# RWKV-7 pairs: the second head's products of three steps on the other column half of TensorE, put back in place by the copies

## The chip, the cores and the metric

One core of one Trainium2 chip runs the whole program as one launch. The metric is the device time of one execution in microseconds (us). Five engines are named as the profile names them: PE (TensorE, matrix products; PEld are its weight loads), DVE (VectorE), ACT (ScalarE), POOL (GpSimd) and SP (which issues the DMAs). A matmul reads a stationary operand and a moving operand from SBUF and writes into one of eight PSUM banks; ACT or DVE then copies the result out.

## The reference

A decoder trunk of two layers over 512 tokens of width 1024. Each layer has a token mixer with three branches (sparse attention NSA, latent attention MLA, RWKV-7 time mixing), merged by gates, and a gated MLP behind it. The change touches the RWKV-7 branch alone: eight heads of width 64 with a state that is carried from token to token:

```python
def step(state, inp):
    r_t, d_t, k_t, v_t, kk_t, a_t = inp
    sa = jnp.einsum('bhij,bhj->bhi', state, -kk_t)
    state = (state * d_t[:, :, None, :] + sa[..., None] * (kk_t * a_t)[:, :, None, :]
             + v_t[..., None] * k_t[:, :, None, :])
    return state, jnp.einsum('bhij,bhj->bhi', state, r_t)
...
_, y = lax.scan(step, state0, xs)
```

The kernel computes the scan in chunks of 64 tokens. Within a chunk the token-by-token recurrence becomes a triangular system, so that nearly everything is a product of 64x64 matrices in f32.

## The kernel before

All instructions of the program come from generator functions ("tasks") that a list scheduler written in the kernel interleaves: at each step it gives the next place to the request that could start first by its own cost table, then by priority (a smaller number goes first). The scheduler fixes the order of each engine's instructions when the program is built. The large matrix products of the projections and the MLP are one task, `master` (priority 9), which walks a list of units in a fixed order (`ORDER`): it fills PE's time wherever the other tasks have nothing ready. Its weights come by DMA, are rounded to a high part by ACT (the CASTs of line 507 into `hlt`) and get a low part by DVE (line 476, `hlt<-rawt,hlt`).

Eight heads make four **pairs** per layer (`rwkv_pair`, spawned by `rwkv_setup`, priority 1, at most three alive at once), so eight pairs in all. A pair holds four blocks `t` of 128 tokens, each two chunks `c` of 64 tokens; chunk `c` lies on partitions 64c to 64c+63 (`cs(c)`). Head `h` of the pair lies along the free axis. The steps of a pair in their order:

- `chunk_mats(2, ..)` and, in the task `left`, `chunk_mats(3, ..)`: products within each chunk, `Ab` and `Ak`, 16 matmuls of 64x64 with 128 columns each. Then in `left`: **X1**, 16 matmuls `Ak` by `v4` with 64 columns, into one bank, copied out by ACT in one instruction.
- `rw_inverse`, beside `left`: inverts the triangular systems.
- **solve**, behind both: 2 tasks, one a head, 8 matmuls each with 128 columns into a bank of their own, copied to `G` with factor -0.5 by ACT or DVE, whichever the scheduler finds free first.
- `mat_rm` and `mat_k`: 32 matmuls each, written through `quad`; beside them **local** (priority 1.5): 32 matmuls (16 pairs that accumulate) into one bank, copied to `Yp` by ACT.
- a scan of six short steps over the chunks, the readout (16 matmuls through `quad`), normalisation, output.

`pe` hands matmuls to PE in pieces of 8, between which other tasks may come. `quad(a, b, 2)` takes two matmuls of list `a`, two of `b`, and so on. PE's array is used as four quadrants here: the partitions of the operands choose the row half, the partitions of the output the column half. In `chunk_mats`, `mat_rm`, `mat_k` and the readout four consecutive matmuls lie in four different quadrants. In X1, solve and local both operands lie on `cs(c)` and the output on `cs(c)` too, so that only the two quadrants on the diagonal are used, whatever the head.

Each f32 matmul stands in the trace as two MATMUL records: the 16 matmuls of X1 are x32, the 32 of local x64.

Of the kernel before, what the change touches and what calls it, by code (L numbers as in the profile page):

```python
# [429 lines left out]
class Kern:  # L430
# [1744 lines left out]
    def rwkv_pair(self, l, st, i):  # L2175
        nc, A = self.nc, self.A
        tts = range(4)
        idn = self.ident()
        name = self.sch.cur.name
# [10 lines left out]
        src = A["rwrow"][l, i]  # L2190
# [9 lines left out]
        cs = lambda c: slice(64 * c, 64 * c + 64)  # L2200
        AR = yield from self.pages(2, None, job)
        al, X1p = self.pg(AR), self.pg(AR + 1)
# [92 lines left out]
        pr = self.sch.cur.prio  # L2295
# [29 lines left out]
        v4 = vv.rearrange("p (t h c) -> p t h c", t=4, h=2)  # L2325
        ka4 = ka.rearrange("p (t h c) -> p t h c", t=4, h=2)
        bt4 = bt.rearrange("p (t h c) -> p t h c", t=4, h=2)
        alx = self.pg(AR, 2).rearrange("p (w t h c) -> p w t h c", w=2, t=4, h=2)
        hct = [(h, t, c) for t in tts for h in range(2) for c in range(2)]
# [3 lines left out]
        Ab = self.pg(AB, 2).rearrange("p (h t w c) -> p h t w c", h=2, t=4, w=2)  # L2333
        Ak = self.pg(AK, 2).rearrange("p (h t w c) -> p h t w c", h=2, t=4, w=2)

        def chunk_mats(q, M, mo):
            T = self.pg(CTs[q])
            bs, os, mm = [], [], [[], []]
            for h in range(2):
                bs.append((yield from self.bank()))  # L2340
                os.append(self.ps[bs[h]].rearrange("p (t w c) -> p t w c", t=4, w=2))
                for t in tts:
                    for c in range(2):
                        tk = slice(t * 128 + 64 * c, t * 128 + 64 * c + 64)
                        mm[h].append((os[h][64 * c:64 * c + 64, t], T[cs(h), tk], arT[cs(h), :, tk], True, True))
            yield from self.quad(*mm, 2)
            for h in range(2):
                self.fork()
                yield from self.tt(M[:, h], os[h], self.kc(mo, 128).rearrange("p (w c) -> p w c", w=2)[:, None]
                                   .to_broadcast([128, 4, 2, 64]), OP.mult)  # L2350
                self.bfree(bs[h])
            self.join()

        yield dn[0]
        yield dn[1]
        self.pfree(P["rho"])

        def left():
            yield dn[3]
            yield from chunk_mats(3, Ak, KP_MK)  # L2360
            self.pfree(CT3)

            b = yield from self.bank()
            o = self.ps[b].rearrange("p (t h c) -> p t h c", t=4, h=2)
            mm = [(o[cs(c), t, h], Ak[cs(c), h, t, 0], v4[cs(c), t, h], True, True) for h, t, c in hct]
            yield from self.pe(mm[:8])
            yield from self.pe(mm[8:])
            yield from self.cp(X1p, self.ps[b], only="ACT")
            self.bfree(b)

        yield dn[2]
        yield from chunk_mats(2, Ab, KP_MB)
        self.pfree(CT2)
        dl = self.spawn(left(), pr, name)

        XT = yield from self.rw_inverse(Ab, i, job)
        yield dl
        self.pfree(CT)
        XTp = self.pg(XT).rearrange("p (h t c) -> p h t c", h=2, t=4)
        GH = yield from self.pages(2, None, job)  # L2380
        G = self.pg(GH, 2).rearrange("p (h t w c) -> p h t w c", h=2, t=4, w=2)

        def solve(h):
            b = yield from self.bank()
            o = self.ps[b].rearrange("p (t w c) -> p t w c", t=4, w=2)
            yield from self.pe([(o[cs(c), t], XTp[cs(c), h, t], alx[cs(c), :, t, h, :], True, True)
                                for t in tts for c in range(2)])
            yield from self.cp(G[:, h], o, scale=-0.5)
            self.bfree(b)

        yield from self.par([solve(h) for h in range(2)], pr, name)
        self.pfree(XT)
        self.pfree(AR, 2)

# [4 lines left out]
        Yp = self.pg(Y)  # L2399
# [40 lines left out]
            self.join()  # L2440

        def local():
            b = yield from self.bank()
            o = self.ps[b].rearrange("p (t h c) -> p t h c", t=4, h=2)
            mm = []
            for h, t, c in hct:
                mm.append((o[cs(c), t, h], Ak[cs(c), h, t, 1], v4[cs(c), t, h], True, False))
                mm.append((o[cs(c), t, h], Ab[cs(c), h, t, 1], G[cs(c), h, t, 1], False, True))
            for q in range(0, 32, 8):
                yield from self.pe(mm[q:q + 8])  # L2450
            yield from self.cp(Yp, self.ps[b], only="ACT")
            self.bfree(b)

        dloc = self.spawn(local(), pr + 0.5, name)
        yield from self.par([mat_rm(), mat_k()], pr, name)

# [5 lines left out]
        for n in range(1, 7):  # L2462
            t, c = divmod(n, 2)
            o = self.ps[bS][:, n * 64:(n + 1) * 64]
# [13 lines left out]
        bs, os, mm = [], [], [[], []]  # L2478
# [37 lines left out]
        b = yield from self.bank()  # L2516
# [5 lines left out]
        b = yield from self.bank()  # L2522
# [250 lines left out]
```

## Time and profile before

| | |
|---|---|
| median of 3 runs | 2071.39 us (2071.12 to 2074.33) |
| the profiled execution, time | 2071.48 us |
| its span in the trace | 2069.4 us |
| PE busy | 2019.6 us (98%) |
| DVE busy | 1340.3 us (65%) |
| ACT busy | 998.2 us (48%) |
| mean granted PE clock | 0.994 |

The time of an execution is its span and some 2 us around it. A busy PE is one with a matmul in its pipeline, so a short and poorly filled matmul counts as much as a full one. The pairs run at about 76 to 404 us (first layer) and 1094 to 1425 us (second layer); behind them come NSA, the output projection and the MLP, which the change doesn't touch.

### The profile page before, as it was taken

How to read it: one execution, taken by the hardware profiler on the slowest of the kernel's cores; microseconds unless marked ns; L12 is line 12 of the kernel's file. 1: busy time of each engine (PE TensorE's matmuls, PEld its weight loads, DVE VectorE, ACT ScalarE, POOL GpSimd, SP SyncE). 2: the span in 40 equal slices, each digit the busy share in tenths (PEclk: the TensorE clock that was granted, in tenths of full speed). 3: DMA queues.
4: the chain of work that ended last, by engine and by line, in shares of the span. 5: the costliest groups of instructions: out<-in, count | busy, mean ns of one | idle time of the engine just before them, and what ended most of it. 6: DMA issues, size and time to landing. Idle time of an engine off the chain costs nothing.

```text
span 2069.4 us, 35607 instructions
## 1 busy us (share of the span) xinstructions
PE 2019.6 (98%) x14134; PEld 1638.0 (79%) x14134; DVE 1340.3 (65%) x2754; ACT 998.2 (48%) x1898; POOL 292.2 (14%) x268
## 2 busy tenths in 40 slices
PE   6999999999999999999999999999999999999998
PEld 4887777777788888888888777777777878888887
DVE  6687985677556766662467789765865676656423
ACT  4454652466445656541344456534754455444321
POOL 3001000340030234200010100004302211100000
PEclk9999999999999999999999999999999999999999
DMA  7532212441245355424422221224313544333342
GB/s 308 152 93 74 72 43 87 153 163 52 99 166 173 123 194 174 141 92 141 138 85 67 66 89 57 75 87 166 129 62 123 173 143 168 108 102 93 101 133 81
DMA packets 88423, 245.48 MB, mean 119 GB/s; under 512 B 24984, under 2 KB 26392, under 8 KB 87872
## 3 DMA queue, kind: packets, MB, share of 16 engines
q1 hardware_dynamic: 88256, 243.20, 35.3%
q8 instruction: 111, 1.82, 0.4%
q14 instruction: 56, 0.46, 0.1%
HBM read 233.19 MB, written 12.60 MB: 119 GB/s over the span
## 4 chain that ended last, share of the span: by engine, by line
PE 88%; DVE 8%; issue 1%; ACT 1%; DMA 1%; POOL 1%; DVEq 0%; POOLq 0%; SPq 0%; ACTq 0%
PE ps L457 83%; PE ps L463 4%; DVE xt L476 1%; DVE xt L485 1%; DVE arena L476 1%; DVE xt L1797 1%; DVE xt L480 1%; DVE hlt L476 1%; ACT xt L472 0%; POOL smallt L517 0%; DVE arena L480 0%; DVE arena L1213 0%; DMA arena<-rwd 0%; DVE xt L2561 0%; DMA rwd<-arena 0%
## 5 line engine op out<-in xcount | busy, mean ns | idle before, releaser
L457 PE MATMUL ps<-arenar,hlt 128*128 128x512 f32 (+1 forms) x2880 | 711.7, 396 | 1.6 <-DVE arenar L476 1.4
L457 PEld LDWEIGHTS ps<-arenar,hlt 128*128 128x128 f32 x2880 | 520.6, 190 | 109.1 <-issue 7.3
L476 DVE TENSOR_TENSOR hlt<-rawt,hlt 128x1024 fp32r<-128x1024 f32 (+2 forms) x260 | 312.6, 1202 | 371.1 <-ACT hlt L507 370.0
L457 PE MATMUL ps<-xt,hlt 128*128 128x512 f32 (+1 forms) x2208 | 477.5, 378 | 4.2 <-ACT arena L1211 4.2
L507 ACT CAST hlt<-rawt 128x1024 fp32r<-128x1024 f32 (+3 forms) x263 | 269.4, 1025 | 431.9 <-PE ps L457 323.0
L457 PEld LDWEIGHTS ps<-xt,hlt 128*128 128x128 f32 x2208 | 397.0, 190 | 81.0 <-ACT arena L1211 4.7
L457 PE MATMUL ps<-hlt,arenar 128*128 128x512 f32 (+3 forms) x1056 | 222.5, 365 | 0.0
L457 PEld LDWEIGHTS ps<-hlt,arenar 128*128 128x128 f32 x1056 | 185.4, 189 | 27.4 <-issue 1.0
L507 ACT COPY xt<-ps 128x512 f32<-128x512 f32 (+6 forms) x211 | 91.0, 476 | 91.6 <-PE ps L457 43.4
L480 DVE SCALAR_TENSOR_TENSOR yt<-ps,cpk,yt 128x511 f32<-128x511 f32 (+1 forms) x160 | 119.5, 747 | 3.3
L457 PE MATMUL ps<-xt 64*64 64x64 f32 (+11 forms) x1992 | 117.1, 258 | 4.3 <-ACT xt L472 2.4
L457 PEld LDWEIGHTS ps<-xt 64*64 64x64 f32 (+6 forms) x1992 | 84.2, 135 | 46.3 <-issue 31.4
L472 ACT ACTIVATE xt<-xt,smallt 128x512 f32<-128x512 f32 (+3 forms) x168 | 92.5, 552 | 55.8 <-DVE smallt L1797 55.7
L517 POOL TENSOR_TENSOR smallt<-smallt,mhalf 128x1 f32<-128x1 f32 (+2 forms) x56 | 58.5, 1049 | 276.3 <-DVE smallt L487 157.1
L457 PE MATMUL ps<-arenar 128*128 128x512 f32 x384 | 93.0, 390 | 0.0
L522 POOL TENSOR_SCALAR smallt<-smallt 128x1 f32<-128x1 f32 x20 | 5.1, 256 | 593.6 <-DVE smallt L487 582.6
L971 POOL TENSOR_TENSOR arena<-xt,arena 128x512 f32<-128x512 f32 x51 | 73.7, 1445 | 71.9 <-issue 36.7
L457 PEld LDWEIGHTS ps<-arenar 128*128 128x128 f32 x384 | 71.7, 188 | 14.7
L463 PE MATMUL ps<-kpack,xt 128*128 128x128 f32 x533 | 73.7, 275 | 6.2 <-DVE xt L476 4.5
L457 PE MATMUL ps<-hlt,xt 128*128 128x512 f32 x336 | 76.8, 389 | 0.0
L463 PEld LDWEIGHTS ps<-kpack,xt 128*128 128x128 f32 x533 | 61.1, 140 | 18.3 <-issue 3.7
L457 PEld LDWEIGHTS ps<-hlt,xt 128*128 128x128 f32 x336 | 63.1, 188 | 13.1
(264 smaller groups left out, 2490.4 us busy)
## 6 DMA issues: line engine op xcount, KB each, us to landing
rawt<-in_wch_dram SPq DMA_DIRECT2D x90, 512.0 KB, 3.5
rawt<-in_wup_dram SPq DMA_DIRECT2D x88, 512.0 KB, 3.5
rawt<-in_wdn_dram SPq DMA_DIRECT2D x44, 512.0 KB, 3.5
arena<-in_wada_dram SPq DMA_DIRECT2D x42, 512.0 KB, 5.2
xt<-in_wada_dram SPq DMA_DIRECT2D x33, 512.0 KB, 5.3
rawt<-in_wbr_dram SPq DMA_DIRECT2D x24, 512.0 KB, 3.5
yt<-in_wada_dram SPq DMA_DIRECT2D x21, 512.0 KB, 4.7
rawt<-in_wout_dram SPq DMA_DIRECT2D x16, 512.0 KB, 3.5
```

The costliest lines, as they stand in the source:

```text
L457: self.nc.tensor.matmul(out, lhsT, rhs, start=st, stop=sp)
L463: self.nc.tensor.transpose(out, in_, ident)
L472: self.nc.scalar.activation(out, in_, func, bias=bias, scale=scale, **kw)
L476: self.nc.vector.tensor_tensor(out, a, b, op)
L480: self.nc.vector.scalar_tensor_tensor(out, a, s, b, op0, op1)
L485: self.nc.vector.tensor_scalar(out, a, s1, None, op0)
L507: self.nc.scalar.copy(out, in_)
L517: self.nc.gpsimd.tensor_tensor(out, in_, ex, OP.pow)
L522: self.nc.gpsimd.tensor_scalar(out, ss, a, b, OP.mult, OP.add)
L971: self.nc.gpsimd.tensor_tensor(a, w, a, OP.add)
L1797: nc.vector.tensor_tensor_reduce(dst, B3(o), B3(mask_ap(qt)), scale, 3.0e38, OP.add, OP.min, sm[:, qt:qt + 1])
```

## The change

A new helper `crossed` takes the place of three pieces of code. It takes two lists of matmuls (one for chunk half `c` = 0, one for `c` = 1), two banks (one for each `c`), and gives them to `quad(.., 2)`. The first head's output goes to partitions `cs(c)`, the second head's to `cs(1-c)`, the other column half. Since the second head's results then lie on the wrong half of the partitions, four copies of 64 partitions (one for each `c` and `h`) bring them back, in place of one or two copies of 128 partitions. X1 and local, which had one bank each, now have two; their copies stay on ACT. Solve's two tasks become one, with two banks as before; its copies may go to ACT or DVE. The number of matmuls and their sizes stay.

```diff
+        def crossed(mm, n, dst, scale, only):
+            bs, os = [], []
+            for c in range(2):
+                bs.append((yield from self.bank()))
+                os.append(self.ps[bs[c]][:, 0:256 * n].rearrange("p (t w c) -> p t w c", t=4, w=n))
+            per = len(mm[0]) // 8
+            yield from self.quad(*[[(os[c][cs(c ^ (q % 2)), q // (2 * per)], *m) for q, m in enumerate(mm[c])]
+                                   for c in range(2)], 2)
+            for c in range(2):
+                for h in range(2):
+                    self.fork()
+                    src = os[c][cs(c ^ h)]
+                    yield from self.cp(dst(c, h), src if n > 1 else src[:, :, 0], scale=scale, only=only)
+            self.join()
+            for b in bs:
+                self.bfree(b)
...
-            b = yield from self.bank()
-            o = self.ps[b].rearrange("p (t h c) -> p t h c", t=4, h=2)
-            mm = [(o[cs(c), t, h], Ak[cs(c), h, t, 0], v4[cs(c), t, h], True, True) for h, t, c in hct]
-            yield from self.pe(mm[:8])
-            yield from self.pe(mm[8:])
-            yield from self.cp(X1p, self.ps[b], only="ACT")
-            self.bfree(b)
+            yield from crossed([[(Ak[cs(c), h, t, 0], v4[cs(c), t, h], True, True) for t in tts for h in range(2)]
+                                for c in range(2)], 1,
+                               lambda c, h: X1p.rearrange("p (t h c) -> p t h c", t=4, h=2)[cs(c), :, h], None, "ACT")
...
-        def solve(h):
-            b = yield from self.bank()
-            o = self.ps[b].rearrange("p (t w c) -> p t w c", t=4, w=2)
-            yield from self.pe([(o[cs(c), t], XTp[cs(c), h, t], alx[cs(c), :, t, h, :], True, True)
-                                for t in tts for c in range(2)])
-            yield from self.cp(G[:, h], o, scale=-0.5)
-            self.bfree(b)
-
-        yield from self.par([solve(h) for h in range(2)], pr, name)
+        yield from crossed([[(XTp[cs(c), h, t], alx[cs(c), :, t, h, :], True, True) for t in tts for h in range(2)]
+                            for c in range(2)], 2, lambda c, h: G[cs(c), h], -0.5, None)
...
         def local():
-            b = yield from self.bank()
-            o = self.ps[b].rearrange("p (t h c) -> p t h c", t=4, h=2)
             mm = []
-            for h, t, c in hct:
-                mm.append((o[cs(c), t, h], Ak[cs(c), h, t, 1], v4[cs(c), t, h], True, False))
-                mm.append((o[cs(c), t, h], Ab[cs(c), h, t, 1], G[cs(c), h, t, 1], False, True))
-            for q in range(0, 32, 8):
-                yield from self.pe(mm[q:q + 8])
-            yield from self.cp(Yp, self.ps[b], only="ACT")
-            self.bfree(b)
+            for c in range(2):
+                mm.append([m for t in tts for m in
+                           [(Ak[cs(c), h, t, 1], v4[cs(c), t, h], True, False) for h in range(2)]
+                           + [(Ab[cs(c), h, t, 1], G[cs(c), h, t, 1], False, True) for h in range(2)]])
+            yield from crossed(mm, 1, lambda c, h: Yp.rearrange("p (t h c) -> p t h c", t=4, h=2)[cs(c), :, h], None, "ACT")
```

The scheduler lays the whole program out anew, so that the order changes nearly everywhere. Two places of the first layer's first pair show the kind of it. On PE, X1 and then solve stand like this before (`ps` is a bank, `hlt,arenar` a large matrix product of `master`, `arena,xt` operands of the pair; x16 are 16 matmuls):

```order
L463 MATMUL ps_76<-kpack,arena 128x128 x4
L457 MATMUL ps_82<-arena,xt_104 64x64 x16
L463 MATMUL ps_77<-kpack,arena 128x128 x4
...
L457 MATMUL ps_79<-hlt,arenar 128x312 x3
L457 MATMUL ps_76<-arena,xt_104 64x128 x8
L457 MATMUL ps_81<-arena,xt_104 64x128 x8
L457 MATMUL ps_77<-hlt,arenar 128x312 x3
```

and like this with the change, where the first four rows are followed by six, and the two of solve by six, that alternate in the same way:

```order
L463 MATMUL ps_76<-kpack,arena 128x128 x4
L457 MATMUL ps_78<-hlt,arenar 128x384 x3
L457 MATMUL ps_82<-arena,xt_104 64x64 x2
L457 MATMUL ps_77<-arena,xt_104 64x64 x2
...
L457 MATMUL ps_78<-hlt,arenar 128x312 x3
L457 MATMUL ps_81<-arena,xt_104 64x128 x2
L457 MATMUL ps_82<-arena,xt_104 64x128 x2
...
L457 MATMUL ps_76<-hlt,arenar 128x312 x3
```

Each step keeps its matmuls and stays one block between large products; what moved is the bank (and with it the quadrant), which changes after every second matmul.

On ACT, around solve and local of the same pair, before (line 509 is a copy with a factor, line 507 a plain one; the two rows of 128x512 by line 509 are solve, `xt_104<-ps_82` is local):

```order
L507 CAST hlt<-rawt 128x1024
L509 ACTIVATE arena<-ps_76 128x512
L509 ACTIVATE arena<-ps_81 128x512
L507 CAST hlt<-rawt 128x768
L507 COPY xt_104<-ps_82 128x512
```

and with the change (the two rows of 64x4x64 are local's four copies):

```order
L509 ACTIVATE xt_104<-ps_81 64x512 x2
L507 CAST hlt<-rawt 128x1024
L507 COPY arena<-ps_80 64x4x64 x2
L507 COPY arena<-ps_83 64x4x64 x2
L507 CAST hlt<-rawt 128x768
```

Solve's other two copies went to DVE, between a step of another pair's inverse and a low part of a weight:

```order
L2565 TENSOR_REDUCE arena<-xt_104 64x15
L513 TENSOR_SCALAR xt_104<-ps_82 64x512 x2
L476 TENSOR_TENSOR hlt<-rawt,hlt 128x1024
L476 TENSOR_TENSOR arena<-ps_80,kpack 128x4x64
L476 TENSOR_TENSOR arena<-ps_80,arena 128x4x64
```

Of solve's 32 copies in the program 20 are on ACT and 12 on DVE (before: 16, all on ACT); X1 and local have 64 on ACT (before: 16).

## Rows read from the trace of the kernel before

**Rows 1.** The page, parts 1 and 4: busy time by engine; the chain by engine.

```profile
PE 2019.6 (98%) x14134; PEld 1638.0 (79%) x14134; DVE 1340.3 (65%) x2754; ACT 998.2 (48%) x1898; POOL 292.2 (14%) x268
...
PE 88%; DVE 8%; issue 1%; ACT 1%; DMA 1%; POOL 1%; DVEq 0%; POOLq 0%; SPq 0%; ACTq 0%
```

**Rows 2.** Busy time by stretch (columns in the first line), the pairs' stretches.

```profile
core 0: us, PE busy (x) PEld busy (x) DVE busy (x) ACT busy (x) POOL busy (x), PEclk, DMA share, GB/s
110.00:200.00 90.00, 87.53 (x1255) 73.92 (x1254) 70.83 (x196) 42.22 (x100) 7.68 (x11) 0.98 0.27 80
200.00:330.00 130.00, 129.90 (x1275) 98.07 (x1273) 108.92 (x291) 70.35 (x162) 7.84 (x9) 1.00 0.22 67
330.00:400.00 70.00, 67.66 (x797) 53.23 (x796) 47.04 (x83) 26.83 (x43) 12.25 (x9) 0.97 0.34 113
1120.00:1200.00 80.00, 77.72 (x1201) 66.44 (x1200) 63.41 (x181) 35.70 (x88) 7.96 (x12) 1.00 0.23 62
1200.00:1350.00 150.00, 150.00 (x1377) 113.34 (x1377) 125.40 (x321) 83.92 (x186) 8.51 (x10) 1.00 0.24 72
1350.00:1400.00 50.00, 49.44 (x765) 38.60 (x761) 31.95 (x68) 18.00 (x32) 1.43 (x2) 1.00 0.31 98
```

**Rows 3.** PE's timeline (start, us, engine, line, what): X1, solve, local, each with its follower.

```profile
225.60 1.15 PE L457 MATMUL ps<-xt 64*64 64x64 f32 x32
226.67 0.97 PE L457 MATMUL ps<-arenar,hlt 128*128 128x512 f32 x3
...
1287.07 1.96 PE L457 MATMUL ps<-arena,xt 64*64 64x128 f32 x32
1288.96 1.31 PE L463 MATMUL ps<-kpack,xt 128*128 128x128 f32 x10
...
174.41 2.13 PE L457 MATMUL ps<-arena,xt 64*64 64x64 f32 x64
176.47 0.96 PE L457 MATMUL ps<-arenar,hlt 128*128 128x512 f32 x3
```

**Rows 4.** PE's timeline: readout, `chunk_mats` and `mat_k`, each with its follower.

```profile
286.45 0.69 PE L457 MATMUL ps<-xt,arena 64*64 64x64 f32 x32
287.08 1.22 PE L457 MATMUL ps<-xt 96*128 96x384 f32 x4
...
1333.95 1.10 PE L457 MATMUL ps<-arena 64*64 64x128 f32 x32
1334.98 2.16 PE L457 MATMUL ps<-xt 128*64 128x512 f32 x12
...
172.24 1.16 PE L457 MATMUL ps<-arena 64*64 64x64 f32 x64
173.33 0.97 PE L457 MATMUL ps<-arenar,hlt 128*128 128x512 f32 x3
```

**Rows 5.** Groups by line and shape: copies out of PSUM on ACT (busy, mean ns).

```profile
L507 ACT COPY arena<-ps 128x512 f32<-128x512 f32 x35 | 19.9, 588 | 24.0 <-PE ps L463 15.9 <-PE ps L457 8.0
L507 ACT COPY xt<-ps 128x256 f32<-128x256 f32 x29 | 11.0, 386 | 0.4
L509 ACT ACTIVATE xt<-ps 128x512 f32<-128x512 f32 x9 | 5.4, 600 | 6.0 <-PE ps L457 6.0
```

**Rows 6.** Line 513, DVE's copies with a factor (ns min/median/max).

```profile
L513 DVE TENSOR_SCALAR arena<-ps x4: 692/692/693, 197.1 to 1356.5; 128x512 f32<-128x512 f32 x4
```

**Rows 7.** PE's waits by releaser, the longest (us in total, times, longest).

```profile
PE ps L463 <- DVE yt L1130: 10.7, 2, 7.8
PE ps L463 <- DVE arena L1185: 6.9, 3, 2.6
PE ps L463 <- DVE xt L476: 4.5, 4, 1.9
```

**Rows 8.** PE's timeline: NSA's last products, and the large products at 593 us.

```profile
555.80 2.38 PE L457 MATMUL ps<-xt,arena 128*64 128x512 f32 x16
...
592.66 7.64 PE L457 MATMUL ps<-arenar,hlt 128*128 128x512 f32 x33
```

**Rows 9.** Busy time by stretch, where the granted clock was low among the pairs.

```profile
133.70:137.00 3.30, 3.30 (x16) 2.98 (x17) 2.29 (x13) 0.51 (x2) 0.00 (x0) 0.50 0.41 150
396.50:403.30 6.80, 6.80 (x30) 5.42 (x29) 0.32 (x2) 1.04 (x2) 0.00 (x0) 0.50 0.74 299
```

**Rows 10.** PE's timeline: idle time ahead of those two stretches (in brackets).

```profile
132.88 0.68 PE L457 MATMUL ps<-xt 64*64 64x64 f32 x16 [2.36 <-ACT xt L472]
...
395.76 0.63 PE L463 MATMUL ps<-kpack,xt 128*128 128x128 f32 x4 [1.95 <-DVE xt L476]
```

**Rows 11.** Timeline, first pair of the first layer: solve on PE, its copies, `mat_rm`.

```profile
146.94 1.96 PE L457 MATMUL ps<-arena,xt 64*64 64x128 f32 x32
...
148.08 0.60 ACT L509 ACTIVATE arena<-ps 128x512 f32<-128x512 f32 x1 [0.66 <-PE ps L457]
...
148.95 0.60 ACT L509 ACTIVATE arena<-ps 128x512 f32<-128x512 f32 x1 [0.28 <-PE ps L457]
...
150.32 0.69 PE L457 MATMUL ps<-xt,arena 64*64 64x64 f32 x32
```

## Prediction

> **What bounds the kernel now.** I read the busy times and the chain first, then the stretches in which the pairs run, then PE's timeline inside them. PE is busy for 2019.6 of 2069.4 us, and the chain that ended last lies on PE for 88% of the span; DVE holds 8% of it, ACT 1% [rows 1]. In the six stretches that hold nearly all of the pairs' work, PE is busy for 562.3 of 570 us. DVE comes next, and never nearer than in 200 to 330 us (108.9 of 130 us, 84%) and 1200 to 1350 us (125.4 of 150, 84%); ACT stays at 56% or less in all of them [rows 2]. PE's longest waits are on DVE at the start of the program and at the norms between the parts of a layer, not on a pair [rows 7]. So in the pairs' stretches PE is the engine that always has something to do: when a pair waits, `master` fills in. There a microsecond of PE work that goes away should come off the end, as long as `master` has units that it may start.
>
> Busy time can't say how well PE is filled, so the next view is the timeline. What a block of matmuls costs PE is the time from its start to the start of the block behind it, since a matmul's own duration is mostly pipeline. X1 takes 226.67 - 225.60 = 1.07 us for 32 records, solve 1288.96 - 1287.07 = 1.89 us for 32 records of 128 columns, local 176.47 - 174.41 = 2.06 us for 64 records [rows 3]. Blocks of the same number and shape that lie in four quadrants are in the same trace: the readout takes 0.63 us for 32 records of 64 columns, `chunk_mats` 1.03 us for 32 of 128 columns, `mat_k` 1.09 us for 64 of 64 columns [rows 4]. From the two blocks of 64 columns on either side, 32 records more cost 0.99 us on the diagonal and 0.46 us over four quadrants: a record costs 31 ns against 14 ns, and about 0.1 to 0.2 us of each block is entering and leaving, which stays.
>
> **What the change does to PE.** The matmuls stay as they are, and each of the three steps gets the arrangement of its counterpart: two matmuls of one row half to both column halves, then two of the other row half, and a bank for each row half. `mat_k` even shares local's pattern of two accumulating products in turn. So I price each step at its counterpart. Per pair: X1 1.07 - 0.63 = 0.44 us, solve 1.89 - 1.03 = 0.86 us, local 2.06 - 1.09 = 0.97 us, together 2.27 us [rows 3, 4]. Eight pairs make 18.2 us. From below: if only the streams shrank and each step were cut into one piece more by work of other tasks, at some 0.15 us a piece, three steps of eight pairs would give back 3.6 us, leaving 14.6 us. From above: local is often cut into pieces before and pays the entry more than once; if half of the pairs lose two such entries, 1.2 us come on top, 19.4 us. I take 18.2 us, which is whole blocks against whole blocks.
>
> **What it adds on ACT and DVE.** No row shows a copy of 64 partitions and 256 columns out of PSUM on ACT; the nearest is 128 partitions by 256 columns at 386 ns, against 588 ns for 512 columns [rows 5]. Halving the columns saves only a third, so four copies of 386 ns in place of one of 588 ns add 0.96 us, for X1 and for local: 1.91 us a pair, 15.3 us in all, on ACT. Solve has 32 copies of 512 columns on half the partitions, which I price as whole ones (600 ns on ACT [rows 5], 692 ns on DVE [rows 6]): 20 on ACT in place of 16 add 2.4 us, 12 on DVE add 8.3 us. Together 26 us of copies. None of it is on PE. ACT goes from 998 to 1016 us and DVE from 1340 to 1349 us, both far from the span. In the tightest stretch, 200 to 330 us, a pair and a half of DVE copies are about 1.6 us on 108.9, with the stretch shorter by 3.4 us: 110.5 of 126.6, or 87%. So I cost the copies at nothing for the end; the cover is `master`'s work on PE while the pair waits.
>
> The rows speak for that, but the Trainium skill has a rule that speaks against the change. "TensorEngine Tiling (Array Packing)", section "Performance Considerations", under "PSUM Bottleneck", says that packing the array speeds up TensorE but not the emptying of PSUM, which can become the bottleneck, and advises copies that take in several tiles at once; this change splits four copies of a pair into twelve. No row of before shows PE held by a pair's copy for long. If the rule decided, it would be the last rival below.
>
> **What it does to a pair's own chain.** X1's four copies run beside the inverse, which takes far longer. Local's run beside the scan. Only solve is on the chain: from its start to `mat_rm` 150.32 - 146.94 = 3.38 us pass, of which 1.89 are PE, and the last copy ends 0.77 us before `mat_rm` starts [rows 11]. With the change PE takes 1.03 us, all four copies wait for the last matmul's group, and two run on each engine or three on one: 1.2 to 1.8 us of copies in place of the 0.6 us behind the second head. That is -0.26 to +0.34 us a pair, nothing either way. X1 and local hold two banks for longer in place of one; a pair that waits for a bank leaves PE to `master`.
>
> **Does the saved time reach the end?** `master` gets ahead of the branches by about 9 us in each layer. Its list makes it wait for a branch's result only where it multiplies that result. The place that I dated is NSA, the last branch: its last products start at 555.8 us and end at 558.2. Between them and the first product that needs NSA the list `ORDER` still has about seven units of 24 matmuls (from Z27 to Z05); at 7.64 us for 33 matmuls a unit takes 5.6 us, so that product stands at some 597 us, within the last row of the group [rows 8]. 39 us of slack are four times 9 us, even if NSA came no sooner. Behind the mixer the work is the same and just starts earlier.
>
> **Clock.** Two stretches among the pairs ran at a granted clock of 0.5, 1.2 in place of 2.4 GHz, behind idle gaps of PE of 2.36 and 1.95 us: 133.7 to 137.0 us and 396.5 to 403.3 us [rows 9, 10]. At the full clock their work takes half, so they cost about 1.7 and 3.4 us. In the new order such gaps may go or others come. I put nothing into the sum and up to 5 us into the range on either side.
>
> **The sum.** 2071.48 us (the profiled execution, 0.1 us over the median) - 18.2 us = 2053.3 us, so 2053 us.
>
> **Rivals.**
>
> First, the saving is partly lost: in 200 to 330 and 1200 to 1350 us DVE, which makes the low part of every weight of `master`, is at 84%, and the new order may bunch it so that PE runs dry now and then. For: these two stretches are the fullest ones [rows 2]. Against: 87% is not 100%, and PE stands still for 0.1 us of 280 us there now. Half of the saving lost gives 2071.5 - 9.1 = 2062 us.
>
> Second, the steps don't run four wide, and nothing changes: 2071 us. The mechanism would be that the second head's weights, on the same row half as the first head's, can't be loaded while the first head's product runs, so that two row halves is all that overlaps. Against it: `chunk_mats` and `mat_k` send both column halves of one row half in a row and cost half as much a record as the diagonal steps [rows 3, 4]. The Trainium skill states that mechanism: "TensorE: Matmul & The Clock Gate", section "Part 3: Packing small matmuls — row/col tiling", says that a weight load overlaps with matmuls in flight only when its row group differs. By that rule the saving would be nothing; the rows of the four-quadrant steps don't agree with it, so it gets a small chance.
>
> Third, slower: the pair's copies hold PE. The place is the stretch in which two or three pairs are alive, where the casts that feed `master` queue behind eight short copies a pair on ACT, and the low parts behind solve's copies on DVE. If PE waited for every added microsecond of copies, the sum would be 2071.5 - 18.2 + 26.0 = 2079 us; it turns slower than before once more than 70% (18.2 of 26.0) of that time reaches PE. For that `master` would have to run with no prepared weight at nearly each of these copies. Against: ACT is busy for 54% and 56% of the fullest stretches and DVE for 84% [rows 2].
>
> **How the numbers follow.** The forecast 0.76 (own range 2047 to 2059: the 14.6 and 19.4 us, and the clock by up to 5 us), partly lost 0.14 (2059 to 2067), nothing 0.05, slower 0.05. The range 2046 to 2061 takes in the forecast and the better part of the second case. About 0.2% or 4 us is what a measurement of this kernel can tell from no change. Faster by more than that: 0.90 (the first two cases); within it 0.05; slower 0.05.
>
> **What would show it.** In the trace of after: X1's 32 records in 0.6 to 0.7 us from start to follower, solve's in about 1.0 us, local's 64 in about 1.1 us; PE's busy time lower by 15 to 20 us and its idle time as before; ACT up by some 18 us and DVE by some 8 us; the output projection of the first layer earlier by about 9 us. I am wrong if the three blocks stay at 1.07, 1.89 and 2.06 us (second rival), or if they shrink while PE's idle time in the pairs' stretches grows by about as much, with waits on ACT or DVE in front of `master`'s matmuls (first or third rival).

## The result and the profile after

The changed kernel takes 2049.2 us (median, 2047.98 to 2050.45), the kernel before 2071.26 us beside it: a ratio of 0.9895 (95% interval 0.9876 to 0.9914), 22.1 us less. The forecast was 2053 us, the range 2046 to 2061. One of the eleven executions of the kernel before with 420 ns, in the experiments below, took 5317 us at a granted clock of 0.375; its median there is 2067.8 us with it and 2067.5 us without it, and its ratio leaves it out.

The page of the changed kernel, parts 1 and 4, against [rows 1]:

```profile
PE 1999.4 (98%) x14134; PEld 1617.0 (79%) x14134; DVE 1345.9 (66%) x2766; ACT 1015.0 (50%) x1950; POOL 296.9 (15%) x268
...
PE 85%; DVE 9%; ACT 2%; issue 2%; POOL 1%; DMA 0%; DVEq 0%; POOLq 0%; ACTq 0%; SPq 0%
```

PE is busy for 20.2 us less, with the same 14134 matmul records. The span fell by 23.2 us, from 2069.4 to 2046.2, so PE's idle time fell too, from 49.8 to 46.8 us, though not among the pairs: there it rose from 9.7 us (103 to 408.5 and 1121 to 1425 us before) to 12.7 us (103 to 405 and 1110 to 1403 us after). ACT rose by 16.8 us (52 copies more), DVE by 5.6 us (12 copies more). PE is still the engine that is never free.

PE's timeline of the changed kernel: X1, solve and local, each with the block behind it, against [rows 3]:

```profile
102.42 0.69 PE L457 MATMUL ps<-arena,xt 64*64 64x64 f32 x32
103.05 0.79 PE L457 MATMUL ps<-hlt,arenar 128*128 128x384 f32 x3
...
144.98 1.10 PE L457 MATMUL ps<-arena,xt 64*64 64x128 f32 x32
146.02 2.40 PE L457 MATMUL ps<-hlt,arenar 128*128 128x312 f32 x15
...
171.55 1.11 PE L457 MATMUL ps<-arena,xt 64*64 64x64 f32 x64
172.59 0.73 PE L457 MATMUL ps<-arenar,hlt 128*128 128x512 f32 x2
```

From start to follower X1 takes 0.63 us (before 1.07), solve 1.04 (1.89), local 1.04 (2.06): these are the times of the blocks that lay over four quadrants already [rows 4]. Summed over the eight pairs, from the start of each of a step's records to the start of the next one and without idle time, X1 fell from 8.7 to 5.0 us, solve from 14.9 to 8.2, local from 17.3 to 10.2: 17.5 us in all.

ACT's copies of 64 partitions and 256 columns, which the trace of before didn't hold, and the two fullest stretches as in [rows 2], the second one taken 10 us earlier:

```profile
L507 ACT COPY xt<-ps 64x256 f32<-64x256 f32 x44 | 16.1, 367 | 20.7 <-PE ps L457 20.3
```

```profile
200.00:330.00 130.00, 127.51 (x1172) 93.05 (x1171) 106.75 (x285) 71.22 (x166) 8.15 (x9) 0.97 0.23 69
1190.00:1340.00 150.00, 149.56 (x1461) 113.05 (x1461) 127.04 (x331) 84.29 (x193) 10.17 (x10) 1.00 0.22 68
```

Half the partitions and half the columns cost 367 ns against 588 for a whole bank [rows 5]. DVE is at 82% and 85% of the two stretches, ACT at 55% and 56%: neither became the bound. In the first one PE now stands still for 2.5 us where it stood for 0.1, and the granted clock, 1.00 before, is 0.97: among waits of 0.80, 0.44 and 0.99 us for copies into `xt`, 6.7 us ran at half clock (1.2 GHz).

```profile
236.60:243.30 6.70, 6.05 (x16) 2.40 (x18) 4.62 (x16) 4.24 (x10) 0.00 (x0) 0.50 0.40 133
```

On PE the three steps account for 17.5 of the 23.2 us; the rest lies elsewhere in the program. One place can be shown whole: the start of the second layer, where the first large products run while the last blocks of tokens are still being normalised. PE's timeline there, before and then after:

```profile
1052.84 5.90 PE L457 MATMUL ps<-arenar,hlt 128*128 128x256 f32 x47 [0.20 <-DVE arenar L476]
1061.32 1.29 PE L463 MATMUL ps<-kpack,arena 128*128 128x128 f32 x8 [2.59 <-DVE arena L1185]
```

```profile
1044.58 8.06 PE L457 MATMUL ps<-arenar,hlt 128*128 128x256 f32 x65 [0.20 <-DVE arenar L476]
1053.07 1.09 PE L463 MATMUL ps<-kpack,arena 128*128 128x128 f32 x8 [0.44 <-DVE arena L1185]
```

The normalisation takes as long as before (1061.32 - 1052.84 = 8.48 us, 1053.07 - 1044.58 = 8.49 us), but the new order put 65 products in front of the transposes where 47 stood, so PE waits 0.44 us in place of 2.59. No pair is at work there. Over the three waits of this kind, at the norms between the parts of a layer, PE's wait fell from 6.9 us [rows 7] to 2.1:

```profile
PE ps L463 <- DVE arena L1185: 2.1, 3, 1.0
```

These 4.8 us aren't work of the three steps. The wait at 1053 us follows the new order (0.42 to 0.45 us in the three runs below that keep it); the other two also change from run to run in one order (all three together 5.1, 3.7 and 2.2 us there). The experiments ask how much of the 22 us is of that kind.

### The profile page after: what moved, and what is told of

It is laid out like the page before. It is cut to its first block, busy times and chain, and to the rows that moved or that the text cites. A ratio compares the mean times of both kernels' runs of the same rounds, so it can differ in the third digit from the quotient of the medians.

```text
span 2046.2 us, 35657 instructions
## 1 busy us (share of the span) xinstructions
PE 1999.4 (98%) x14134; PEld 1617.0 (79%) x14134; DVE 1345.9 (66%) x2766; ACT 1015.0 (50%) x1950; POOL 296.9 (15%) x268
## 4 chain that ended last, share of the span: by engine, by line
PE 85%; DVE 9%; ACT 2%; issue 2%; POOL 1%; DMA 0%; DVEq 0%; POOLq 0%; ACTq 0%; SPq 0%
PE ps L457 81%; PE ps L463 4%; DVE xt L476 2%; DVE arena L476 1%; DVE xt L1797 1%; POOL smallt L517 1%; DVE xt L480 1%; ACT xt L472 1%; DVE xt L485 1%; DVE hlt L476 0%; DVE arena L2565 0%; ACT xt L507 0%; DVE arena L480 0%; DVE smallt L491 0%; DVE arena L1213 0%
## 5 line engine op out<-in xcount | busy, mean ns | idle before, releaser
L472 ACT ACTIVATE xt<-xt,smallt 128x512 f32<-128x512 f32 x192 | 105.8, 553 | 62.0 <-DVE smallt L1797 61.7
L507 ACT COPY xt<-ps 128x512 f32<-128x512 f32 (+7 forms) x238 | 96.6, 443 | 78.9 <-PE ps L463 43.8
L971 POOL TENSOR_TENSOR arena<-xt,arena 128x512 f32<-128x512 f32 x58 | 86.3, 1488 | 154.4 <-ACT xt L472 121.0
L457 PE MATMUL ps<-xt 64*64 64x64 f32 (+9 forms) x2080 | 97.8, 255 | 7.1 <-ACT arenar L507 2.8
L457 PEld LDWEIGHTS ps<-xt 64*64 64x64 f32 (+3 forms) x2080 | 67.5, 134 | 44.7 <-issue 30.8
L463 PE MATMUL ps<-kpack,xt 128*128 128x128 f32 x605 | 84.9, 277 | 3.0 <-ACT xt L507 1.8
L463 PEld LDWEIGHTS ps<-kpack,xt 128*128 128x128 f32 x605 | 69.0, 141 | 14.4 <-ACT xt L507 2.3
```

Source lines behind the costliest of these rows:

```text
L457: self.nc.tensor.matmul(out, lhsT, rhs, start=st, stop=sp)
L463: self.nc.tensor.transpose(out, in_, ident)
L472: self.nc.scalar.activation(out, in_, func, bias=bias, scale=scale, **kw)
L507: self.nc.scalar.copy(out, in_)
L971: self.nc.gpsimd.tensor_tensor(a, w, a, OP.add)
```

## The experiments

**Theory 1**: the gain is the streaming of the three steps over four quadrants, microsecond for microsecond, since PE is the bound; what is over is the order. **Rivals**: the order (or the two banks) gives the gain; or the copies and waits eat or make part of it. All medians stand beside runs of the kernel before on the same chip, 2070.9 to 2071.5 us.

**The changed kernel's order with straight steps.** Order, banks in number, and the twelve copies stay; the second head's products go back to the diagonal.

```diff
-                os.append(self.ps[bs[c]][:, 0:256 * n].rearrange("p (t w c) -> p t w c", t=4, w=n))
+            for h in range(2):
+                os.append(self.ps[bs[h]][:, 0:256 * n].rearrange("p (t w c) -> p t w c", t=4, w=n))
...
-            yield from self.quad(*[[(os[c][cs(c ^ (q % 2)), q // (2 * per)], *m) for q, m in enumerate(mm[c])]
-                                   for c in range(2)], 2)
+            yield from self.quad(*[[(os[q % 2][cs(c), q // (2 * per)], *m) for q, m in enumerate(mm[c])]
+                                   for c in range(2)], 1)
...
-                    src = os[c][cs(c ^ h)]
+                    src = os[h][cs(c)]
```

> The changed kernel with its order of instructions, two banks and four copies a step kept, but with the second head's products back on the diagonal quadrants (a bank for each head, the row halves in turn). Theory 1 (the gain is the streaming over four quadrants): X1 goes back to about 1.07 us from start to follower, solve to 1.89, local to 2.06; PE busy rises by some 17 us over the changed kernel and the time to about 2049 + 17.6 = 2067 us, within 0.3% of the kernel before. Rival (the gain comes from the new order or from a bank for each step's half): the time stays within 4 us of 2049 us.

Measured: 2058.3 us, ratio 0.9937 (0.9923 to 0.995). The blocks went back as theory 1 says; PE's timeline of this run:

```profile
101.99 1.15 PE L457 MATMUL ps<-arena,xt 64*64 64x64 f32 x32
103.07 0.44 PE L457 MATMUL ps<-hlt,arenar 128*128 128x384 f32 x1
...
144.64 1.96 PE L457 MATMUL ps<-arena,xt 64*64 64x128 f32 x32
146.54 0.70 PE L457 MATMUL ps<-hlt,arenar 128*128 128x312 f32 x3
...
173.27 2.05 PE L457 MATMUL ps<-arena,xt 64*64 64x64 f32 x64
175.25 0.97 PE L457 MATMUL ps<-arenar,hlt 128*128 128x512 f32 x3
```

1.08, 1.90 and 1.98 us: two banks and four copies don't shorten a step, the quadrants do. In all the three steps take 40.1 us against 23.4 in the changed kernel, 16.7 more. But the time rose by 9.1 us, not 17: the forecast of 2067 us was missed. The cores' rows of the changed kernel and of this one show one part of the account, the clock:

```profile
core 0: 2046.2 us, clock 0.993
```

```profile
core 0: 2056.5 us, clock 0.996
```

Within its span the changed kernel has 27.9 us at half clock, this one 16.0; by that alone this one would be some 6 us faster. But these are two single executions. Over all of them the mean clock is 0.994 (four) and 0.996 (five), some 4 us, and the four times of the changed kernel don't follow their clocks (2047.98 us at 0.993, 2050.45 at 0.995). The pairs of the second layer settle it better, since both kernels run there at the full clock. Busy time from one matmul to the same one in the other kernel, columns as in [rows 2], the changed kernel and then this one:

```profile
1110.18:1403.09 292.91, 287.78 (x3435) 225.81 (x3434) 238.09 (x592) 157.83 (x349) 34.59 (x33) 1.00 0.28 85
```

```profile
1114.75:1412.83 298.08, 295.78 (x3435) 234.37 (x3434) 238.34 (x592) 156.45 (x349) 33.81 (x33) 1.00 0.27 84
```

The three steps take 8.4 us more here (20.1 against 11.7) and the stretch 5.2 us more; PE's idle time is 2.3 us in place of 5.1. So at one order and one clock some three fifths of what the quadrants save come off the time, and a third goes into waits of PE among the pairs. The longest of these, in the last pair's scan, before the same matmuls in the changed kernel and in this one:

```profile
1374.33 0.33 PE L457 MATMUL ps<-xt 64*64 64x64 f32 x4 [2.54 <-DVE xt L511]
```

```profile
1384.07 0.33 PE L457 MATMUL ps<-xt 64*64 64x64 f32 x4 [0.71 <-DVE xt L511]
```

In the first layer's pairs (from 103.05 to 405.13 us there and 103.07 to 408.34 here) the steps differ by 7.9 us and the stretch by 3.2; there PE's idle time is 2 us less than in the changed kernel, and the changed kernel has 6.8 us more at half clock. So the 17 us of the blocks are there, but in this order only 9 of them reach the end; waits and the clock take most of the rest. And this kernel, whose steps are hardly shorter than before, is still 13 us faster than the kernel before: by this run 13 of the 22 us come with the order, the banks and the copies, and 9 with the quadrants.

**One step at a time.** X1 alone, solve alone, local alone crossed (the three hunks of the diff, one each).

> Only X1 crossed, solve and local as before. Theory 1: X1's blocks from 8.7 to 5.0 us in all, so 2071.3 - 3.7 = 2067.6 us. Rival (the new order decides): anywhere within 8 us of 2071, with no relation to X1's blocks.

> Only solve crossed. Theory 1: solve's blocks from 14.9 to 8.2 us in all, so 2071.3 - 6.7 = 2064.6 us. Rival (the new order decides): anywhere within 8 us of 2071.

> Only local crossed. Theory 1: local with the two steps beside it (mat_rm, mat_k) from 35.8 to about 28.5 us in all, so 2071.3 - 7.3 = 2064 us. Rival (the new order decides): anywhere within 8 us of 2071. By theory 1 the three parts add up to 17.7 us, some 4 us less than the whole change measured.

Measured: X1 alone 2074.4 us, ratio 1.0018 (1.0009 to 1.0026); solve alone 2058.4 us, 0.9941 (0.9928 to 0.9953); local alone 2054.0 us, 0.9918 (0.9906 to 0.9931). Each step's own blocks fell as forecast: X1's from 8.7 to 5.2 us, solve's from 14.9 to 8.1, local's from 17.3 to 9.75. The times don't follow them, and none of the three forecasts of theory 1 (2067.6, 2064.6 and 2064 us) was met: X1 alone is 3 us slower than before, the other two are 6 and 10 us faster than their blocks. The profile of X1 alone has PE idle for 48.6 us up to its last matmul (before 43.6) and 34.8 us at half clock within its span (before 24.2). A saving of 4 us can't be read from the time of a kernel whose order is made anew.

**The same order with more PE work.** The changed kernel, its three steps' matmuls issued twice, which the scheduler isn't told; the order of everything else is the same.

```diff
-        for out, lhsT, rhs, st, sp in mms:
+        for out, lhsT, rhs, st, sp in mms * again:
             self.nc.tensor.matmul(out, lhsT, rhs, start=st, stop=sp)
```

> The changed kernel with its order kept, but the matmuls of X1, solve and local issued twice in a row (the second time writes the same results again). That adds PE streaming and nothing else: 32 records at 14.6 ns, 32 at 27.5 ns and 64 at 14.6 ns a pair, 2.3 us, 18 us in all. Theory 1 (PE is the bound among the pairs, so that each microsecond of its work there reaches the end): 2049 + 18 = 2067 us, give or take 4 us for the clock. Rival (much of what PE is relieved of there goes into waits): less than half of it, under 2058 us.

Measured: 2070.2 us, 21.0 us over the changed kernel (ratio to the kernel before 0.9997, 0.9988 to 1.0006). The page has 1024 records more and PE busy for 16.1 us more:

```profile
PE 2015.5 (98%) x15158; PEld 1634.2 (79%) x15158; DVE 1344.7 (65%) x2766; ACT 1017.2 (49%) x1950; POOL 295.8 (14%) x268
```

By blocks the steps take 42.5 us, 19.1 more than the 23.4. So 19 us of PE work, put into the pairs and nowhere else, come out as 21 us at the end (19.0 between the two profiled spans). That rejects the rival by which less than half would. But not all of it is that work. PE's waits behind nothing that the profile shows, in the changed kernel and then in this one:

```profile
PE ps L457 <- issue: 2.0, 3, 1.3
```

```profile
PE ps L457 <- issue: 6.8, 7, 2.5
```

The 4.8 us more lie nearly all inside the doubled local blocks; what PE waits for there stays open. Without them 16 of the 19 us remain, and the straight kernel, in the same order too, gave 9 of 17. So PE's work in the pairs is on the path for the larger part, but not for each microsecond: some of what the change took off became waits.

**What an order alone is worth.** One number of the scheduler's table (its delay from ACT to PE) changed in both kernels; and the kernel before with the scheduler told that the three steps are as short as crossed ones.

```diff
-    "ACT": {"PE": 380.0, "ACT": 213.0, "DVE": 235.0, "POOL": 235.0, "SP": 150.0},
+    "ACT": {"PE": 420.0, "ACT": 213.0, "DVE": 235.0, "POOL": 235.0, "SP": 150.0},
```

> The kernel before, with one number of the scheduler's cost table changed (the delay that it reckons from ACT to PE, 420 in place of 380 ns): the same work in another order, 791 lines of PE's order differ. It shows what an order alone is worth. Theory 1: within 8 us of 2071 us, either way. Rival (the order of the kernel before is a bad one, and nearly any other is faster by some 10 us): 2058 to 2064 us.

> The changed kernel with the same number changed in the scheduler's cost table. Theory 1: within 8 us of 2049 us, and 17 us below the kernel before with the same number, give or take 8 us. Rival (the order of the changed kernel is a lucky one): 2056 us or more.

> The kernel before, whose scheduler is told that X1, solve and local cost 0.55 of what they do, as for crossed steps: the old arrangement, banks and copies in an order planned for shorter steps. Theory 1: the three steps stay at 41 us on PE, time within 8 us of 2071 us. Rival (the new order by itself is worth half of the gain, as the run with straight steps suggests): 2058 to 2062 us.

And the changed kernel with the scheduler told that the three steps take as long as before:

```diff
-            yield from self.pe(mms[i:i + 8], 0.55)
+            yield from self.pe(mms[i:i + 8], share)
...
-                                   for c in range(2)], 2)
+                                   for c in range(2)], 2, 1.0)
```

> The changed kernel, whose scheduler is told that the three steps take as long on PE as they did before (share 1 in place of 0.55): the work is the same, the order is planned for slower steps. Theory 1 (streaming over four quadrants, 17 us, plus what the order happens to give): the three steps stay at some 23 to 24 us in all, time 2049 us give or take 8 us for the order alone. Rival (the scheduler's smaller cost for the steps is what gives the order its gain): 2058 us or more, with PE idle for 5 us or more beyond the changed kernel's 41 us.

Measured: the kernel before with 420 ns 2067.8 us, ratio 0.9981 (0.9972 to 0.999); planned as if cheap 2079.5 us, 1.0043 (1.0028 to 1.0058). The changed kernel with 420 ns 2053.2 us, 0.9916 (0.9902 to 0.9931); planned at the old cost 2049.4 us, 0.9903 (0.9886 to 0.992). So this order planned for shorter steps is worth nothing by itself (some 9 us slower on the old steps, outside of both expectations), while the straight kernel's order, planned for shorter steps too, is 13 us faster: such a plan can go either way. An order planned for longer steps costs the crossed ones nothing. The old steps in three orders take 2067.8, 2071.3 and 2079.5 us, mean 2072.9; the crossed steps in three orders 2049.2, 2049.4 and 2053.2, mean 2050.6. That is 22 us apart; with the straight kernel (2058.3 us) as a fourth order of the old steps it is 2069.2 against 2050.6, 19 us. No order of the crossed steps is slower than any of the old ones. Within one arrangement an order moves the time by several us either way, and the two kernels of the same 420 ns are 14.6 us apart.

**The copies twice.** Each of a pair's twelve copies done twice in a row, in an order that the scheduler makes with them.

```diff
                     yield from self.cp(dst(c, h), src if n > 1 else src[:, :, 0], scale=scale, only=only)
+                    yield from self.cp(dst(c, h), src if n > 1 else src[:, :, 0], scale=scale, only=only)
```

> The changed kernel, with each of the twelve copies of a pair done twice: 96 copies more, some 36 us on ACT and 8 us on DVE. Theory 1 (the copies lie under PE's other work): PE's busy time as with the change, time 2049 us, give or take 5 us for the new order. Rival (a good part of the copies reaches PE): 2049 + 20 to 40 us.

Measured: 2061.1 us, ratio 0.9954 (0.9941 to 0.9966): 12 us over the changed kernel, between the two forecasts. ACT has 26 us and DVE 22 us more (36 and 8 were expected); PE's busy time is 2001.0 us, 1.6 more. The rest is waiting; PE's timeline at the two longest new waits of the pairs (the first pair's inverse, the product with the gate near the end of the first layer's fourth pair):

```profile
142.96 0.69 PE L457 MATMUL ps<-xt 32*32 32x32 f32 x32 [3.92 <-DVE xt L2599]
...
410.04 1.64 PE L457 MATMUL ps<-xt 128*128 128x128 f32 x8 [3.54 <-DVE arena L480]
```

A quarter of the added copy time reached the end, or part of it is the order, whose spread is as large; this run doesn't tell them apart. "The copies cost nothing" isn't shown. They may have taken a few us of what the steps gave.

**Row halves in turn.** The changed kernel with `quad(.., 1)` in the three steps, which alternates the row halves; all other engines keep their order.

> The changed kernel, with the matmuls of the three steps sent row half by row half in turn (first head of c=0, first head of c=1, second head of c=0, ..) in place of two of one row half and two of the other; the order on all other engines is the same. Theory 1 (four quadrants stream at once, however they follow each other): the three steps' blocks stay as they are with the change (5.0, 8.2 and 10.2 us in all), time within 4 us of 2049 us. Rival (a weight load can't overlap with a product on its own row half, so that the changed kernel pays for pairs on one row half): the blocks get shorter, by up to a quarter, 2 to 6 us in all.

Measured: 2048.0 us, ratio 0.9891 (0.9875 to 0.9906), 1.2 us under the changed kernel with ranges that overlap. The three steps take 5.00, 8.17 and 10.18 us in all, the changed kernel 5.00, 8.18 and 10.18. PE's timeline of this run, X1 and solve with their followers:

```profile
102.54 0.69 PE L457 MATMUL ps<-arena,xt 64*64 64x64 f32 x32
103.16 0.79 PE L457 MATMUL ps<-hlt,arenar 128*128 128x384 f32 x3
...
143.61 1.10 PE L457 MATMUL ps<-arena,xt 64*64 64x128 f32 x32
144.64 2.40 PE L457 MATMUL ps<-hlt,arenar 128*128 128x312 f32 x15
```

Between these two orders of the quadrants it makes no difference: two products in a row on one row half cost no more than row halves in turn.

**One step further.** The changed kernel with the inverse's first product crossed as well; its mask multiplication on DVE becomes four instructions.

```diff
-        mm = [(o[cs(c), h, t], A_[cs(c), h, t], X[cs(c), h, t], True, True) for h, t, c in hct]
-        yield from self.pe(mm[:8])
-        yield from self.pe(mm[8:])
-        yield from self.tt(Pm, o, lv(0), OP.mult)
+        yield from four(cs, 64, lambda c, h, t: A_[cs(c), h, t], lambda c, h, t: X[cs(c), h, t],
+                        lambda c, h, o: self.tt(Pm[cs(c), h], o, self.kc(KP_LV, 64)[cs(c ^ h)][:, None, :]
+                                                .to_broadcast([64, 4, 64]), OP.mult))
```

> The changed kernel, with the inverse's first product (16 matmuls of 64x64 a pair) crossed in the same way; its mask multiplication on DVE, one instruction of 512 columns, becomes four of 64 partitions and 256 columns. Theory 1: the inverse falls from 27.2 to about 23.6 us on PE, DVE has some 7 us more, time 2049 - 3.6 = 2045.6 us, give or take 5 us for the order. Rival (DVE, which is fullest beside the pairs, becomes the bound): PE waits on DVE in the pairs' stretches, and the time stays at 2049 us or rises.

Measured: 2049.1 us, ratio 0.9896 (0.9881 to 0.9912), the same as the changed kernel. The inverse fell from 27.2 to 24.0 us on PE, nearly as forecast, and PE's busy time with it:

```profile
PE 1994.0 (97%) x14134; PEld 1613.4 (79%) x14134; DVE 1362.8 (67%) x2797; ACT 1011.6 (49%) x1943; POOL 295.2 (14%) x268
```

DVE has 16.9 us more (7 were expected), and PE's idle time is 52.1 us in place of 46.8: the 5.4 us that PE is less busy are idle now. 3.4 us of that are at the norms, where no pair is at work; they wait 5.5 us in place of 2.1:

```profile
PE ps L463 <- DVE yt L1185: 2.9, 1, 2.9
...
PE ps L463 <- DVE arena L1185: 2.6, 2, 2.1
```

Here nothing is won. The larger part of the loss isn't in the pairs, so the forecast rival (DVE as the bound there) doesn't explain it, and the waits at the norms come to 5.1 us in a kernel with the changed order too (the straight one); how much DVE's added work and the new order each did stays open.

## Why the prediction was right

**The bound** was read rightly: PE, among the pairs. The kernel with doubled matmuls shows it without a change of order (19 us of work, 21 us of time, 5 of them waits inside the doubled blocks). That a microsecond which goes away comes off the end is too strong: with the order kept, the straight kernel shows 9 of 17 us, and 5.2 of 8.4 us where the clock is full in both. The rest went mostly into PE's waits among the pairs, which the prediction put at nothing, and into the clock. One reading was off as well: the third row of [rows 7], 4.5 us, is mostly two waits ahead of a pair's last transposes (1.95 us at 395.8 [rows 10] and 1.94 at 1418.4), so pairs did hold PE a little before, too.

**The price of each step** was its counterpart over four quadrants. X1 was put at 3.5 us for eight pairs and gave 3.7, solve at 6.9 and gave 6.7, local at 7.8 and gave 7.15, cut in pieces as it was in either kernel: 17.5 us in place of 18.2. This is the part of the prediction that the runs bear out best.

**The copies** were priced at 17.7 us on ACT and 8.3 on DVE; the two engines rose by 16.8 and 5.6. "Nothing for the end" is the step that the runs don't bear out in full: doubled copies cost 12 us, though in another order.

**The chain** of a pair stayed: from solve's start to `mat_rm` the first pair takes 148.35 - 144.98 = 3.37 us after 3.38 before [rows 11], inside the -0.26 to +0.34 us that were worked out. PE's timeline of the changed kernel:

```profile
148.35 0.69 PE L457 MATMUL ps<-xt 64*64 64x64 f32 x32
```

**The slack** held: the second layer's first large products start 8.3 us earlier (1044.58 against 1052.84), about the 9 us that were forecast for the first layer's share.

**What was missing** is a term for the order. The sum gave 18.2 us and the time fell by 22.1. The prediction allowed for the clock alone, 5 us on either side, and took the rest of the program for unchanged. The runs show old and crossed steps each over 4 to 12 us by order only, through PE's idle time at places like the second layer's start and through the time at half clock, which ranges, within the span, from 13.3 us (before with 420 ns) to 34.8 us (X1 alone) for nearly the same work. That the result lies 4 us under the forecast is of that size and no evidence on the steps. That it lies so near is in part luck: a loss to waits and clock that the sum didn't have, and a gain by the order that it didn't have either, nearly cancel. The mean over orders, 19 to 22 us, is near the forecast too, but few orders were tried.

**The rivals.** The first, a saving partly lost, has some truth in it: of the two stretches of full DVE the first has 2.4 us more of idle time and 6.7 us at half clock in the changed kernel, some 5 us together, and the second next to nothing. It doesn't show in the time, which other places of the new order made up for. The steps do run four wide, with the row halves in turn or not. The copies didn't hold PE enough to turn the sign: doubling them left the kernel 10 us faster than the one before.

## What to carry to other kernels

Where a profile shows PE as the bound and small matmuls on two of four quadrants, price them by a block of the same shape that already uses four, from its start to the start of its follower; that price held to within 10% for each of three steps. It is the price on PE; how much of it reaches the end is another question, and the two runs that kept the order gave 9 of 17 us and 16 of 19. Putting results on the wrong partitions and letting the copies bring them back paid off here, with ACT at 55% and DVE at 85% of the fullest stretches; the same trick on a product whose result the pair waits for, with DVE doing more for it, gave nothing in the one order that was tried. In a program whose order a scheduler makes anew, a change of a few us can't be judged by one time: keep the order and change one thing, or try several orders of both kernels.

## What the runs showed of the hardware

- Matmuls of 64x64 in f32 with 64 columns cost PE about 31 ns a record on the two diagonal quadrants and 14 ns over four [rows 3, 4], and the same over four in either of the two orders tried (X1 5.00 us in all, local 10.18).
- A copy out of PSUM by ACT of 64 partitions and 256 columns takes 367 ns, one of 128 partitions and 512 columns 588 ns: splitting one into four costs 2.5 times as much engine time.
- At the full clock and in one order, 8.4 us less of PE work in the second layer's pairs made their stretch 5.2 us shorter; PE's idle time there rose from 2.3 to 5.1 us.
- PE stood still for 1.30 us in the middle of local of the first layer's fourth pair, behind nothing that the profile shows; what it waited for stays open. PE's timeline of the changed kernel:

```profile
366.86 0.22 PE L457 MATMUL ps<-xt 64*64 64x64 f32 x1
368.38 0.34 PE L457 MATMUL ps<-xt 64*64 64x64 f32 x7 [1.30 <-issue]
```
